# Hybrid two-layer trunk on one core: first block sums and two weights' low parts issued behind a norm's last turn on VectorE, and two HGRN transposes moved to another PSUM bank

## The chip, the core and the metric

The kernel runs on one core of a Trainium2 chip. A core has engines that run side by side, each with its own instruction queue: TensorE (PE, with weight loads shown apart as PEld) multiplies and transposes matrices, VectorE (DVE) and ScalarE (ACT) do elementwise work, SyncE (SP) issues the DMA transfers here, and GpSimd (POOL) is almost idle. The on-chip memory SBUF holds tiles of 128 partitions. TensorE writes into PSUM, which is divided into banks of 128 x 512 fp32 numbers; in this kernel a bank is one buffer of a pool.

The metric is the device time of one execution in microseconds (us). Lower is better. All times below are us unless marked otherwise.

## The reference: what is computed

Two layers over x of 512 tokens x 1024 features. Layer 0 mixes tokens by a Mamba-2 SSD mixer, layer 1 by an HGRN2 mixer with 8 heads. After each mixer come a residual layer norm, an MLP with squared ReLU (1024 to 4096 to 1024), another residual layer norm, and a gated per-layer embedding:

```python
for i in range(DEPTH):
    mix = ssd_mixer(x, ...) if i % 2 == 0 else hgrn2_mixer(x, ...)
    h = layer_norm(DEEPNORM_ALPHA * x + mix, ln_g[i, 0], ln_b[i, 0])
    h = layer_norm(DEEPNORM_ALPHA * h + sq_relu_mlp(h, mlp_w1[i], mlp_w2[i]), ln_g[i, 1], ln_b[i, 1])
    x = h + jax.nn.sigmoid(h @ ple_w_gate[i]) * (p[i] @ ple_w_proj[i])
```

An HGRN2 head carries a 128 x 128 state along the sequence. Its output is the product of decayed scores with the values inside a chunk, plus the query times the state carried in; then it is normalised per head and gated, and the heads are projected back to 1024 features.

## The kernel before

**Precision.** Each large product is done in a reduced-precision fp32 format with a split of both operands into a high and a low part. `unit` (L102) loads a 128 x 1024 weight tile into one of three `raw` buffers (issued by SP, L106), ACT casts it to its high part `whi` (L113), and DVE subtracts for the low part `wlo` (L115). `mm3` then makes three matmul passes: high by high (L119), and the two mixed ones (L120, L121). A `raw` buffer is free again when its `wlo` is through, so the load of weight n + 3 waits for the low part of weight n.

**Norms.** There are four, numbered 0 and 1 in layer 0, 2 and 3 in layer 1. A norm works on four chunks of 128 tokens. DVE takes the statistics (norm 0: L207, L208; norm 2: sums that come with the residual addition, L257, then ACT squares, L215), then scales in two passes (L223, L224). `transpose_split` then turns a chunk: for each half `q` of the features, PE makes four 128 x 128 transposes into the one bank of pool `pst`, named "pt" (L233), ACT casts the high part out of it (L237) and DVE subtracts for the low part (L238). I write a turn c0q0 for chunk 0, half 0, up to c3q1.

**MLP.** `mlp_and_gate` goes in periods. In the first period the first four tiles of w1 are multiplied in two token halves: tokens 0 to 255 need only the turns of chunks 0 and 1, tokens 256 to 511 those of chunks 2 and 3. Each tile takes 24 half passes of 256 columns for each half, 96 for the four tiles. The other tiles take 24 full passes of 512 columns. The second product (w2) is done by a block scheme with seven instead of eight products; `weight_sums` makes the sums of weight blocks on DVE (L327, L329, L330, L333) in eight `r` tiles, loaded by SP at L321, which also are weights of the second period.

**HGRN2.** The heads are done in four groups of two, `r` = 0 and 1. Group by group, with names of the code: the keys of each head (`kk`) are turned by PE (L1077, bank "pt") and copied out by ACT as `kt` (L1079); the states are `kt` times the values (L1089: head 0 in "pm", the one bank of pool `psm`, head 1 in a bank of `psy`); outputs are computed (L1107, L1109), normalised by DVE (L1117, L1119), turned (L1127, bank "pt") and split by ACT (L1128) and DVE (L1129) for the output projection. L981 is a product of the scores' part of the next group, fed by DVE through L955 and L956.

**Order of the work.** In the HGRN part the order on PE is written by hand: a group yields after each step the amount of other matmuls (projections) that is put behind it. Elsewhere a scheduler orders each engine's queue from priorities; `high_priority` moves instructions ahead (offset `SOON` = 40 for the turns' splits, `SUMS[0]` = 60 for the first block sums, `LEAD` = 100 for weights). On each engine the queue then runs in this order, and a waiting instruction holds those behind it.

Of the kernel before, what the change touches and what calls it, by code (L numbers as in the profile page):

```python
# [1 line left out]

# [1 line left out]

# [21 lines left out]
LEAD = 100  # L26
# [18 lines left out]
def trunk(ctx: ExitStack, tc, a):  # L45
# [53 lines left out]
        return v.to_broadcast(shape)  # L99


    def unit(src, lead=LEAD):  # L102
        n = src.shape[1]
        with tc.high_priority(offset=lead):
            raw = mk(raws, [P, 1024], "raw")
            nc.sync.dma_start(raw[:, :n], src)  # L106
        return split(raw[:, :n], lead)

    def split(f, lead=LEAD):
        n = f.shape[1]  # L110
        with tc.high_priority(offset=lead):
            hi = mk(whip, [P, 1024], "whi", F32R)
            nc.scalar.copy(hi[:, :n], f)  # L113
            lo = mk(wlop, [P, 1024], "wlo", F32R)
            nc.vector.tensor_sub(lo[:, :n], f, f32(hi[:, :n]))  # L115
        return hi, lo

    def mm3(out, sh, sl, mh, ml, start, stop, **kw):
# [80 lines left out]
    def layer_norm(i, c, gb, sums=None):  # L199
# [23 lines left out]
        nc.vector.scalar_tensor_tensor(src, src, mv[:, 0:1], gb[0], shift, ALU.mult)  # L223
        nc.vector.scalar_tensor_tensor(src, src, rs, gb[1], ALU.mult, ALU.add)  # L224

    def transpose_split(src, dst, c):

        sl = slice(c * P, (c + 1) * P)
        for q in range(2):
            pt = bank(pst, "pt")  # L230
            for j in range(4):
                k = 4 * q + j
                nc.tensor.transpose(pt[:, j * P : (j + 1) * P], src[:, k * P : (k + 1) * P], ident)  # L233
            v = pt.rearrange("p (j t) -> p j t", j=4)
            h = dst.hi[q][:, :, sl]
            with tc.high_priority(offset=SOON):
                nc.scalar.copy(h, v)  # L237
                nc.vector.tensor_sub(dst.lo[q][:, :, sl], v, f32(h))  # L238
            yield

    def out_part(units, n, xs, c, h, first, scale, last=False, sums=None):
# [70 lines left out]
        put("s1", a22)  # L312
        put("s4", a12)

    def weight_sums(w, lead, eng=nc.vector):

        t = [[None, None] for _ in range(4)]

        def load(i, u, src):
            t[i][u] = tmp("r", [P, 1024])  # L320
            nc.sync.dma_start(t[i][u], src)  # L321

        with tc.high_priority(offset=lead):
            for u in range(2):
                load(0, u, w[0][1][u])
                load(2, u, w[1][1][u])
                eng.tensor_sub(t[2][u], t[2][u], t[0][u])  # L327
                load(1, u, w[0][0][u])
                eng.tensor_sub(t[0][u], t[0][u], t[1][u])  # L329
                eng.tensor_add(t[1][u], t[2][u], t[1][u])  # L330
            for u in range(2):
                load(3, u, w[1][0][u])
                eng.tensor_sub(t[3][u], t[3][u], t[1][u])  # L333
        return t

    def block_product(w, blk, lead, first, after=None, turns=None, sums=None):

        t1, t2, t3, t4 = weight_sums(w, lead)  # L340
        seen = set() if first else {(i, j) for i in range(2) for j in range(2)}
        banks = {}

        def product(x, f, name, start, i, j, turns=None):
            us = [split(v) if f in (t1, t2, t3, t4) else unit(v) for v in f]
            if start:
                banks[name] = [bank(psy, "py%d" % c) if name == "x" else bank(psj, "pj") for c in range(2)]
            t = blk[x]
            for c in range(2):
                ps = banks[name][c]  # L350
                sl = slice(c * P, (c + 1) * P)
                for k in range(4):
                    hi, lo = us[k // 2]
                    ks = slice((k % 2) * 512, (k % 2 + 1) * 512)
                    w_ = hi[:, ks], lo[:, ks]
                    mm3(ps, t[:, 0, k, sl], t[:, 1, k, sl], *w_, start and k == 0, k == 3, skip_group_check=True)
                    if turns and (c, k) in ((0, 3), (1, 1)):
                        next(turns)
                d = acc[:, 2 - 2 * i + c, j * 512 : (j + 1) * 512]
                with tc.high_priority(offset=SOON if after else 0):  # L360
                    if after and f in (w[1][0], t1, t4, w[1][1]):
                        nc.vector.tensor_tensor_reduce(
                            d, ps, d, 1.0, 0.0, ALU.add, ALU.add, sums[:, 2 - 2 * i + c, j : j + 1]
                        )
                    elif (i, j) in seen:
                        nc.vector.tensor_add(d, ps, d)
                    else:
                        nc.vector.scalar_tensor_tensor(d, d, ALPHA, ps, ALU.mult, ALU.add)
            seen.add((i, j))

        p1 = lambda: product("a11", w[0][0], "x", True, 0, 0)
        p2 = lambda: product("a12", w[1][0], "z", True, 0, 0)
        p6 = lambda: product("s2", t2, "x", False, 1, 0)
        p7 = lambda: product("s3", t3, "y", True, 1, 1)
        p5 = lambda: product("s1", t1, "x", False, 1, 1)
        p4 = lambda: product("a22", t4, "y", False, 1, 0)
        p3 = lambda: product("s4", w[1][1], "x", False, 0, 1, turns)
        for f in (p1, p7, p6, p4, p5, p2, p3) if after else (p1, p2, p6, p7, p5, p4, p3):
            f()
            if after and f is p5:  # L380
                after(0), after(1)
            if after and f is p3:
                after(2), after(3)
            yield

    def mlp_and_gate(layer, h_s, last):

        w1, w2 = a[f"w1_{layer}"], a[f"w2_{layer}"]
        blocks = {}

        def hidden(g):
            names = ("a11", "a12", "a22", "s1", "s2", "s3", "s4")
            blocks[g] = {
                n: tmp("blk", [P, 2, 4, 256], F32R) if n in ("s3", "s4") else mk(b8, [P, 2, 4, 256], "b8", F32R)
                for n in names
            }
            for p in range(2):
                tiles = [4 * (2 * g + r) + 2 * p + i for r in range(2) for i in range(2)]
                us = []
                if g == p == 0:  # L400
                    for m in tiles:
                        us.append((unit(w1[m]), bank(psj, "pj")))
                        project(us[-1][0], h_s, us[-1][1], tok=slice(0, 256))
                zs = []
                for r in range(2):
                    z = mk(w4, [P, 2, T], "ab"[r])
                    for i in range(2):
                        if us:
                            u, ps = us[2 * r + i]
                            project(u, h_s, ps, tok=slice(256, 512))  # L410
                        else:
                            ps = bank(psj, "pj")
                            project(unit(w1[tiles[2 * r + i]]), h_s, ps)
                        nc.scalar.activation(z[:, i], ps, AF.Relu)
                        if i == 1:
                            nc.scalar.activation(z, z, AF.Square)
                            zs.append(z)
                            if r == 1:
                                half_blocks(blocks[g], *zs, p)
                        yield  # L420

        for g, period in enumerate(PERIODS):
            if g < 4:
                tiles = hidden(g)
            if g > 0:
                if g == 4:
                    h_s, after, turned, sums = norm(2 * layer + 1)
                    p_s = (mk(w4, [P, 2, T], "a", F32R), mk(w4, [P, 2, T], "b", F32R))
                    praw = mk(raws, [P, 1024], "raw")
                    nc.sync.dma_start(praw, a[f"pT_{layer}"].rearrange("p k t -> p (k t)"))  # L430
                    praw = praw.rearrange("p (k t) -> p k t", k=2)
                    nc.scalar.copy(p_s[0], praw)
                    nc.vector.tensor_sub(p_s[1], praw, f32(p_s[0]))
                w = [[[w2[8 * g - 8 + 4 * i + 2 * j + u] for u in range(2)] for j in range(2)] for i in range(2)]
                products = block_product(w, blocks.pop(g - 1), SUMS[g - 1], g == 1, *((after, turned(0), sums) if g == 4 else ()))
            for op in period:
                next(tiles if op == "T" else products)

# [500 lines left out]
    def hcore(h0, s, i0):  # L939
# [132 lines left out]

        kt = []
        for r in R:
            pt = bank(pst, "pt")
            for c in range(3):
                nc.tensor.transpose(pt[:, c * P : (c + 1) * P], kk[r][:, c * P : (c + 1) * P], ident)  # L1077
            kt.append(tmp("btok", [P, 3, P]))
# [5 lines left out]
        sg = lambda c, r: res[c // 2][:, c % 2, 256 + r * P : 256 + (r + 1) * P]  # L1084
        sv = []
        for r in R:
            pss = py(1) if r else bank(psm, "pm")
            for c in range(3):
                nc.tensor.matmul(pss[:, c * P : (c + 1) * P], kt[r][:, c, :], v(c, r), start=True, stop=True)  # L1089
            sv.append(tmp("pv", [P, 3, P]))  # L1090
# [31 lines left out]
            os.append(o)  # L1122
            yield FILL[3]
        for r in R:
            pt = bank(pst, "pt")
            for c in range(NCH):
                nc.tensor.transpose(pt[:, c * P : (c + 1) * P], os[r][:, c, :], ident)  # L1127
            nc.scalar.activation(s.h(i0 + r), pt, AF.Copy, scale=hnw[:, 0:1])  # L1128
# [141 lines left out]
```

## Time and profile before

| what | value |
|---|---|
| median of 3 runs | 1424.9 us (1424.33 to 1425.1) |
| the profiled execution | 1426.6 us, of it 1424.8 in the span of the profile |
| granted TensorE clock | 1.0 |
| TensorE matmuls | 1413.6 us busy, 99% |
| VectorE | 1057.4 us, 74% |
| ScalarE | 754.5 us, 53% |

A row of a timeline gives the start and the duration in us, the engine, the line, the operation, the tile written and the tiles read, how many instructions the row holds, and in brackets the idle time before it with what ended it. A row of the waits of an engine gives the line that waited, the instruction that ended the wait, the total, the number of waits and the longest. Tiles named "b" written at L237 and L238 are the turned chunks.

### The profile page before, as it was taken

How to read it: one execution, taken by the hardware profiler on the slowest of the kernel's cores; microseconds unless marked ns; L12 is line 12 of the kernel's file. 1: busy time of each engine (PE TensorE's matmuls, PEld its weight loads, DVE VectorE, ACT ScalarE, POOL GpSimd, SP SyncE). 2: the span in 40 equal slices, each digit the busy share in tenths (PEclk: the TensorE clock that was granted, in tenths of full speed). 3: DMA queues.
4: the chain of work that ended last, by engine and by line, in shares of the span. 5: the costliest groups of instructions: out<-in, count | busy, mean ns of one | idle time of the engine just before them, and what ended most of it. 6: DMA issues, size and time to landing. Idle time of an engine off the chain costs nothing.

```text
span 1424.8 us, 20421 instructions
## 1 busy us (share of the span) xinstructions
PE 1413.6 (99%) x8061; PEld 1174.6 (82%) x8061; DVE 1057.4 (74%) x1760; ACT 754.5 (53%) x1134; POOL 1.8 (0%) x12
## 2 busy tenths in 40 slices
PE   9999999999999999999999999999999999999998
PEld 7888888888888888888888887887898888888887
DVE  7988687787967667677986576678685867667873
ACT  6776454563265454545545547655555454544641
POOL 0000000000000000000000000000000000000000
PEclk9999999999999999999999999999999999999999
DMA  8432323333433444444621321222163444444231
GB/s 298 142 130 92 119 89 119 104 107 126 152 119 121 158 130 153 133 148 163 215 82 49 133 90 60 75 90 90 50 232 104 148 137 145 148 133 163 89 118 45
DMA packets 49392, 178.02 MB, mean 125 GB/s; under 512 B 5521, under 2 KB 6289, under 8 KB 49169
## 3 DMA queue, kind: packets, MB, share of 16 engines
q1 hardware_dynamic: 49296, 176.73, 36.8%
q8 instruction: 63, 1.03, 0.3%
q14 instruction: 33, 0.26, 0.1%
HBM read 174.54 MB, written 2.16 MB: 124 GB/s over the span
## 4 chain that ended last, share of the span: by engine, by line
PE 94%; DVE 3%; ACT 2%; DMA 1%; issue 0%; SPq 0%; ACTq 0%; DVEq 0%
PE pj L119 23%; PE pj L120 23%; PE pj L121 23%; PE py L119 5%; PE py L121 5%; PE py L120 5%; PE py L735 1%; PE py L741 1%; PE py L981 1%; PE pm L705 1%; DVE wlo L115 1%; PE pt L233 1%; PE pt L693 1%; DMA r<-in_w 1%; PE py L1107 0%
## 5 line engine op out<-in xcount | busy, mean ns | idle before, releaser
L113 ACT CAST whi<-raw 128x1024 fp32r<-128x1024 f32 x222 | 233.0, 1052 | 330.3 <-PE pj L120 234.1
L119 PE MATMUL pj<-b,whi 128*128 128x512 f32 (+1 forms) x1006 | 382.1, 381 | 0.7 <-ACT b L237 0.7
L120 PE MATMUL pj<-b,whi 128*128 128x512 f32 (+1 forms) x1006 | 380.6, 379 | 1.0 <-DVE b L238 1.0
L121 PE MATMUL pj<-b,wlo 128*128 128x512 f32 (+1 forms) x1006 | 379.2, 377 | 0.0
L115 DVE TENSOR_TENSOR wlo<-raw,whi 128x1024 fp32r<-128x1024 f32 x222 | 269.8, 1220 | 142.2 <-ACT whi L113 136.8
L120 PEld LDWEIGHTS pj<-b,whi 128*128 128x128 f32 x1006 | 189.4, 188 | 34.2 <-DVE b L238 1.2
L119 PEld LDWEIGHTS pj<-b,whi 128*128 128x128 f32 x1006 | 188.9, 188 | 34.1 <-ACT b L237 0.9
L121 PEld LDWEIGHTS pj<-b,wlo 128*128 128x128 f32 x1006 | 189.2, 188 | 33.6
L121 PE MATMUL pj<-whi,b 128*128 128x512 f32 x544 | 212.8, 392 | 0.0
L119 PE MATMUL pj<-whi,b 128*128 128x512 f32 x536 | 212.7, 397 | 0.0
L120 PE MATMUL pj<-wlo,b 128*128 128x512 f32 x536 | 210.2, 393 | 0.0
L121 PEld LDWEIGHTS pj<-whi,b 128*128 128x128 f32 x544 | 102.1, 188 | 20.9
L119 PEld LDWEIGHTS pj<-whi,b 128*128 128x128 f32 x536 | 100.7, 188 | 20.6 <-ACT b L1128 0.6
L120 PEld LDWEIGHTS pj<-wlo,b 128*128 128x128 f32 x536 | 100.8, 188 | 19.4
L113 ACT CAST whi<-r 128x1024 fp32r<-128x1024 f32 x72 | 75.7, 1053 | 67.8 <-PE pj L121 38.6
L115 DVE TENSOR_TENSOR wlo<-r,whi 128x1024 fp32r<-128x1024 f32 x72 | 87.6, 1219 | 23.8 <-ACT whi L113 23.2
L121 PE MATMUL py<-whi,b 128*128 128x512 f32 (+1 forms) x250 | 96.9, 388 | 0.0
L120 PE MATMUL py<-wlo,b 128*128 128x512 f32 x224 | 87.2, 389 | 0.0
L119 PE MATMUL py<-whi,b 128*128 128x512 f32 x224 | 87.1, 390 | 0.0
L121 PEld LDWEIGHTS py<-whi,b 128*128 128x128 f32 x250 | 46.9, 188 | 9.7
L634 DVE SCALAR_TENSOR_TENSOR cv<-pj,cst,cv 128x509 f32<-128x509 f32 (+2 forms) x66 | 48.7, 744 | 3.6 <-ACT cv L631 2.8
L119 PEld LDWEIGHTS py<-whi,b 128*128 128x128 f32 x224 | 42.1, 188 | 9.1 <-DVE sg L494 0.3
(303 smaller groups left out, 1864.7 us busy)
## 6 DMA issues: line engine op xcount, KB each, us to landing
raw<-in_w SPq DMA_DIRECT2D x112, 512.0 KB, 3.3
r<-in_w SPq DMA_DIRECT2D x64, 512.0 KB, 3.4
raw<-in_wssd SPq DMA_DIRECT2D x36, 512.0 KB, 3.4
a<-csd SPq DMA_DIRECT2D x16, 512.0 KB, 3.6
raw<-in_wso SPq DMA_DIRECT2D x16, 512.0 KB, 3.3
raw<-in_wg SPq DMA_DIRECT2D x16, 512.0 KB, 3.4
raw<-in_whq SPq DMA_DIRECT2D x16, 512.0 KB, 3.3
raw<-in_whvg SPq DMA_DIRECT2D x14, 512.0 KB, 3.2
```

Source lines behind the costliest of these rows:

```text
L113: nc.scalar.copy(hi[:, :n], f)
L115: nc.vector.tensor_sub(lo[:, :n], f, f32(hi[:, :n]))
L119: nc.tensor.matmul(out, sh, mh, start=start, stop=False, **kw)
L120: nc.tensor.matmul(out, sh, ml, start=False, stop=False, **kw)
L121: nc.tensor.matmul(out, sl, mh, start=False, stop=stop, **kw)
L233: nc.tensor.transpose(pt[:, j * P : (j + 1) * P], src[:, k * P : (k + 1) * P], ident)
L634: nc.vector.scalar_tensor_tensor(cv[:, d:], ps[:, : T - d], convw[:, i, k : k + 1], cv[:, d:], ALU.mult, ALU.add)
L693: nc.tensor.transpose(pt[:, c * P : (c + 1) * P], xs[:, c * P : (c + 1) * P], ident)
L705: nc.tensor.matmul(pst_[:, c * P : (c + 1) * P], btok[:, c, :], xw[:, c].rearrange("p h q -> p (h q)"), start=True, stop=True)
L735: nc.tensor.matmul(yd[64 * r : 64 * r + 64, sl], xdt[:, 2 * c + r, :], m[:, r, sl], start=True, stop=True)
L741: nc.tensor.matmul(yo[:, c * P : (c + 1) * P], pv[:, c - 1].rearrange("p h q -> p (h q)"), cm[:, c * P : (c + 1) * P], start=True, stop=True,)
L981: nc.tensor.matmul(pcs[r][bs, at : at + n], kk[r][:, ts], qs, start=True, stop=True)
```

## The change

Two edits that touch different stages.

First, `transpose_split` remembers the last DVE subtraction that it issued. `mlp_and_gate`, which is called after all four chunks of norm 0 or norm 2 have been written down, keeps that instruction as `low`, the low part of turn c3q1. `tc.issue_after(low)` tells the scheduler to put an instruction behind `low` in its engine's queue. It is used for all block sums of the first group (eight tiles, on DVE) and for the low parts of the fifth and sixth weight tile of the first period. Their loads and the ACT casts are not held.

Second, in each HGRN group the second head's key turn and the second head's output turn go to bank "pm" in place of "pt", and the first head's states to "pt" in place of "pm".

```diff
+    turned_last = []
+
+    def behind(ins):
+        return tc.issue_after(ins.ins) if ins is not None else nullcontext()
...
                 nc.scalar.copy(h, v)
-                nc.vector.tensor_sub(dst.lo[q][:, :, sl], v, f32(h))
+                turned_last[:] = [nc.vector.tensor_sub(dst.lo[q][:, :, sl], v, f32(h))]
...
             lo = mk(wlop, [P, 1024], "wlo", F32R)
-            nc.vector.tensor_sub(lo[:, :n], f, f32(hi[:, :n]))
+            with behind(after):
+                nc.vector.tensor_sub(lo[:, :n], f, f32(hi[:, :n]))
...
                 load(2, u, w[1][1][u])
-                eng.tensor_sub(t[2][u], t[2][u], t[0][u])
+                with behind(after):
+                    eng.tensor_sub(t[2][u], t[2][u], t[0][u])
...
+        low = turned_last[0]
...
-                            project(unit(w1[tiles[2 * r + i]]), h_s, ps)
+                            project(unit(w1[tiles[2 * r + i]], after=low if g == 0 and r == 0 else None), h_s, ps)
...
         for r in R:
-            pt = bank(pst, "pt")
+            pt = bank(psm, "pm") if r else bank(pst, "pt")
             for c in range(3):
...
-            pss = py(1) if r else bank(psm, "pm")
+            pss = py(1) if r else bank(pst, "pt")
...
         for r in R:
-            pt = bank(pst, "pt")
+            pt = bank(psm, "pm") if r else bank(pst, "pt")
             for c in range(NCH):
```

The scheduler moves more than the held instructions. The queue of DVE at the end of norm 0, before (L238 and L224 are the turns' low parts and the second scaling pass; `wlo` are weights' low parts; the `r` rows are block sums):

```order
L115 TENSOR_TENSOR wlo_3643<-raw_3639,whi_3641 128x1024
L221 RECIPROCAL lnrs_3362<-lnsd_3356 128x1
L223 SCALAR_TENSOR_TENSOR acc_99<-acc_99,lnmv_3355,a_3124 128x1024
L238 TENSOR_TENSOR b_554_3131<-pt_3320,b_552_3129 128x4x128
L224 SCALAR_TENSOR_TENSOR acc_99<-acc_99,lnrs_3362,b_3125 128x1024
L115 TENSOR_TENSOR wlo_3675<-raw_3671,whi_3673 128x1024
L327 TENSOR_TENSOR r_3871<-r_3871,r_3869 128x1024
L238 TENSOR_TENSOR b_553_3130<-pt_3366,b_551_3128 128x4x128
L329 TENSOR_TENSOR r_3869<-r_3869,r_3874 128x1024
L333 TENSOR_TENSOR r_3878<-r_3878,r_3865 128x1024
L238 TENSOR_TENSOR b_554_3131<-pt_3373,b_552_3129 128x4x128
```

and after the change (lines are ten or fewer higher: L244 is L238, L225 is L224, L116 is L115, L334 is L327):

```order
L222 RECIPROCAL lnrs_3362<-lnsd_3356 128x1
L224 SCALAR_TENSOR_TENSOR acc_99<-acc_99,lnmv_3355,a_3124 128x1024
L244 TENSOR_TENSOR b_554_3131<-pt_3320,b_552_3129 128x4x128
L225 SCALAR_TENSOR_TENSOR acc_99<-acc_99,lnrs_3362,b_3125 128x1024
L244 TENSOR_TENSOR b_553_3130<-pt_3366,b_551_3128 128x4x128
L244 TENSOR_TENSOR b_554_3131<-pt_3373,b_552_3129 128x4x128
L116 TENSOR_TENSOR wlo_3643<-raw_3639,whi_3641 128x1024
L116 TENSOR_TENSOR wlo_3675<-raw_3671,whi_3673 128x1024
L334 TENSOR_TENSOR r_3862<-r_3862,r_3860 128x1024
```

The fifth and sixth weight's low parts and all sums now follow the last turn. Three sums (L327, L329, L330) that stood among the steps of chunks 0 to 2 have moved there as well. On PE the turn c3q0 now stands behind 65 half passes of the first token half instead of all 96, with 13 half passes between it and c3q1 (4 before).

ACT's queue in norm 0, before (L237 is a turn's cast, L209 the square root; the last `whi` row is the sixth weight):

```order
L113 CAST whi_3641<-raw_3639 128x1024
L237 CAST b_552_3129<-pt_3267 128x4x128
L209 ACTIVATE lnsd_3303<-lnmv_3302,cst_167 128x1
L113 CAST whi_3673<-raw_3671 128x1024
L237 CAST b_551_3128<-pt_3313 128x4x128
```

and after:

```order
L210 ACTIVATE lnsd_3303<-lnmv_3302,cst_167 128x1
L113 CAST whi_3486<-raw_3484 128x1024
L113 CAST whi_3641<-raw_3639 128x1024
L113 CAST whi_3673<-raw_3671 128x1024
L243 CAST b_551_3128<-pt_3313 128x4x128
```

Here the turn's cast of chunk 1 (the second row before) has moved ahead of the weights' casts, and three weights' casts stand in a row ahead of chunk 2's first turn cast.

DVE's queue at the end of norm 2, before:

```order
L238 TENSOR_TENSOR b_1398_9048<-pt_9235,b_1396_9046 128x4x128
L224 SCALAR_TENSOR_TENSOR acc_99<-acc_99,lnrs_9280,b_9042 128x1024
L238 TENSOR_TENSOR b_1397_9047<-pt_9284,b_1395_9045 128x4x128
L327 TENSOR_TENSOR r_9780<-r_9780,r_9778 128x1024
L238 TENSOR_TENSOR b_1398_9048<-pt_9291,b_1396_9046 128x4x128
```

and after:

```order
L225 SCALAR_TENSOR_TENSOR acc_99<-acc_99,lnrs_9280,b_9042 128x1024
L244 TENSOR_TENSOR b_1397_9047<-pt_9284,b_1395_9045 128x4x128
L244 TENSOR_TENSOR b_1398_9048<-pt_9291,b_1396_9046 128x4x128
L116 TENSOR_TENSOR wlo_9561<-raw_9557,whi_9559 128x1024
L116 TENSOR_TENSOR wlo_9593<-raw_9589,whi_9591 128x1024
L334 TENSOR_TENSOR r_9780<-r_9780,r_9778 128x1024
```

The sum that stood between the last two turns' low parts is behind them. On SP five loads of `r` tiles now go ahead of the eighth and ninth weight's loads (seven went behind them before). In the HGRN part the order on PE is unchanged but in the last group, where the second output turn is spread in pieces among matmuls; only the banks differ.

More of the change, by code (lines that the diff above doesn't have):

```diff
@@ L1 @@
-from contextlib import ExitStack
+from contextlib import ExitStack, nullcontext
 import numpy as np
@@ L99, in bc, with unit @@
         return v.to_broadcast(shape)
-    def unit(src, lead=LEAD):
+    def unit(src, lead=LEAD, after=None):
         n = src.shape[1]
@@ L106, in unit, with split @@
             nc.sync.dma_start(raw[:, :n], src)
-        return split(raw[:, :n], lead)
-    def split(f, lead=LEAD):
+        return split(raw[:, :n], lead, after)
+    def split(f, lead=LEAD, after=None):
         n = f.shape[1]
@@ L313, in half_blocks, with weight_sums @@
         put("s4", a12)
-    def weight_sums(w, lead, eng=nc.vector):
+    def weight_sums(w, lead, eng=nc.vector, after=None):
         t = [[None, None] for _ in range(4)]
@@ L326, in weight_sums, with block_product @@
                 load(2, u, w[1][1][u])
-                eng.tensor_sub(t[2][u], t[2][u], t[0][u])
+                with behind(after):
+                    eng.tensor_sub(t[2][u], t[2][u], t[0][u])
                 load(1, u, w[0][0][u])
-                eng.tensor_sub(t[0][u], t[0][u], t[1][u])
-                eng.tensor_add(t[1][u], t[2][u], t[1][u])
+                with behind(after):
+                    eng.tensor_sub(t[0][u], t[0][u], t[1][u])
+                    eng.tensor_add(t[1][u], t[2][u], t[1][u])
             for u in range(2):
                 load(3, u, w[1][0][u])
-                eng.tensor_sub(t[3][u], t[3][u], t[1][u])
-        return t
-    def block_product(w, blk, lead, first, after=None, turns=None, sums=None):
-        t1, t2, t3, t4 = weight_sums(w, lead)
+                with behind(after):
+                    eng.tensor_sub(t[3][u], t[3][u], t[1][u])
+        return t
+    def block_product(w, blk, lead, first, after=None, turns=None, sums=None, low=None):
+        t1, t2, t3, t4 = weight_sums(w, lead, after=low)
         seen = set() if first else {(i, j) for i in range(2) for j in range(2)}
@@ L434, in mlp_and_gate @@
                 w = [[[w2[8 * g - 8 + 4 * i + 2 * j + u] for u in range(2)] for j in range(2)] for i in range(2)]
-                products = block_product(w, blocks.pop(g - 1), SUMS[g - 1], g == 1, *((after, turned(0), sums) if g == 4 else ()))
+                products = block_product(w, blocks.pop(g - 1), SUMS[g - 1], g == 1, *((after, turned(0), sums) if g == 4 else ()), low=low if g == 1 else None)
             for op in period:
```

## The prediction

> **What bounds the kernel now.** I read the page first, then the waits of TensorE (PE), then the timelines of the five places where a wait stands.
>
> ```profile
> span 1424.8 us, 20421 instructions
> PE 1413.6 (99%) x8061; PEld 1174.6 (82%) x8061; DVE 1057.4 (74%) x1760; ACT 754.5 (53%) x1134; POOL 1.8 (0%) x12
> ```
>
> PE is busy 99% of the span, and its granted clock is full in all forty slices. The instructions of PE stay the same work, so the change can only move the time in which PE waits. That time is listed whole:
>
> ```profile
> PE pt L1127 <- DVE b L1129: 1.5, 2, 1.0
> PE pm L153 <- DVE sq L150: 1.4, 1, 1.4
> PE pt L1077 <- ACT btok L1079: 1.4, 1, 1.4
> PE pj L120 <- DVE b L238: 1.0, 1, 1.0
> PE pj L119 <- ACT b L237: 0.7, 1, 0.7
> PE pt L233 <- DVE b L238: 0.6, 1, 0.6
> PE py L981 <- DVE qd L956: 0.4, 1, 0.4
> ```
>
> Apart from the start (L153), every large wait is at a place that the change touches: L1077 and L1127 are the HGRN turns that get another bank, L237 and L238 the last turns of the norms. A wait costs a little more than its idle time, since the end of a matmul is modelled; I count from start to start and subtract a steady step, which for a 512-column matmul is 0.23 (below, 861.38 to 861.61), for a 256-column one half of that, 0.12, and for a transpose 0.10 (863.40 to 863.71 is three).
>
> **HGRN, the second head's kk turn (group 1).** Both turns wrote bank "pt", so the second waited until ACT had copied the first out.
>
> ```profile
> 861.38 0.39 PE L120 MATMUL pj<-b,whi 128*128 128x512 f32 x1
> 861.61 0.40 PE L121 MATMUL pj<-b,wlo 128*128 128x512 f32 x1
> 863.40 0.55 PE L1077 MATMUL pt<-cst,cv 128*128 128x128 f32 x3 [1.39 <-ACT btok L1079]
> 863.71 0.48 PE L119 MATMUL pj<-b,whi 128*128 128x512 f32 x1
> 861.80 1.04 ACT L113 CAST whi<-raw 128x1024 fp32r<-128x1024 f32 x1
> 862.87 0.48 ACT L1079 COPY btok<-pt 128x384 f32<-128x384 f32 x1
> ```
>
> The loss is 863.40 - 861.61 - 0.23 = 1.56. ACT reaches the copy late, behind a weight cast. In "pm" the turn can start at 861.84. Six matmuls follow it, then the first head's states, which read that copy: 861.84 + 0.31 + 6 x 0.23 = 863.5, against the copy's end at 862.87 + 0.48 = 863.35. The wait is thus covered by six matmuls that were behind it, with 0.15 to spare; that the states now write "pt" adds only a dependence on the same copy. I take 1.5; the ends are 0.2 (the states wait instead) and 1.56. The three other groups show no wait at L1077: nothing.
>
> **HGRN, the second head's output turn (groups 2 and 3).** The same, but behind the DVE's low part of the first turn.
>
> ```profile
> 923.47 0.60 DVE L1119 SCALAR_TENSOR_TENSOR cbm<-py,hri,b 128x128 f32<-128x128 f32 x2
> 925.12 0.75 DVE L1129 SCALAR_TENSOR_TENSOR b<-pt,cst,b 128x512 fp32r<-128x512 f32 x1
> 925.06 0.39 PE L121 MATMUL pj<-b,wlo 128*128 128x512 f32 x1
> 925.92 0.66 PE L1127 MATMUL pt<-cst,cbm 128*128 128x128 f32 x4 [0.47 <-DVE b L1129]
> ```
>
> Loss 925.92 - 925.06 - 0.23 = 0.63. With its own bank the turn needs only the outputs of 923.47, done at 924.07, so it starts at 925.29. Gain 0.6.
>
> ```profile
> 970.40 0.60 DVE L1119 SCALAR_TENSOR_TENSOR cbm<-py,hri,b 128x128 f32<-128x128 f32 x2
> 972.19 0.75 DVE L1129 SCALAR_TENSOR_TENSOR b<-pt,cst,b 128x512 fp32r<-128x512 f32 x1 [1.18 <-ACT b L1128]
> 971.58 0.39 PE L121 MATMUL pj<-whi,b 128*128 128x512 f32 x1
> 972.99 0.66 PE L1127 MATMUL pt<-cst,cbm 128*128 128x128 f32 x4 [1.02 <-DVE b L1129]
> ```
>
> In group 3 the loss is 972.99 - 971.58 - 0.23 = 1.18, and the outputs are done at 971.0. But the DVE work ahead of the next intra-chunk product (L981, which already waits 0.4 for L956) runs through its own queue from 972.19 on, and comes earlier only by what ACT lets it; about half of the gain then returns as a longer wait at L981. I take 0.6, between 0.5 and 1.2. Together HGRN gives 1.5 + 0.6 + 0.6 = 2.7.
>
> **Norm 0: what leaves DVE's queue.** These rows stand between the chunks' steps; after, only the low parts of the third and fourth weight stay.
>
> ```profile
> 361.14 1.21 DVE L327 TENSOR_TENSOR r<-r,r 128x1024 f32<-128x1024 f32 x1
> 366.62 1.17 DVE L330 TENSOR_TENSOR r<-r,r 128x1024 f32<-128x1024 f32 x1
> 373.74 1.21 DVE L115 TENSOR_TENSOR wlo<-raw,whi 128x1024 fp32r<-128x1024 f32 x1
> 381.68 1.17 DVE L115 TENSOR_TENSOR wlo<-raw,whi 128x1024 fp32r<-128x1024 f32 x1
> 384.63 1.27 DVE L224 SCALAR_TENSOR_TENSOR acc<-acc,lnrs,b 128x1024 f32<-128x1024 f32 x1
> 388.09 0.68 DVE L238 TENSOR_TENSOR b<-pt,b 128x512 fp32r<-128x512 f32 x1
> 386.16 0.60 PE L233 MATMUL pt<-cst,acc 128*128 128x128 f32 x4
> 387.43 0.75 PE L119 MATMUL pj<-b,whi 128*128 128x256 f32 x4 [0.67 <-ACT b L237]
> 388.82 0.55 PE L233 MATMUL pt<-cst,acc 128*128 128x128 f32 x3 [0.65 <-DVE b L238]
> ```
>
> PE loses 387.43 - 386.16 - 4 x 0.10 = 0.87 behind the first turn of chunk 3, because all 96 half passes of the chunks before are used up, and before the second 388.82 - 0.10 (the record of its first transpose is missing) - 387.43 - 4 x 0.12 = 0.81. That is 1.7. After, three block sums (the first and the last stand above; 1.2 each, of which the next start hides a little: 3.4) and one low part (381.68, 1.1) no longer stand ahead of chunk 3's L224: it may start 4.5 earlier, at 380.1, and its first turn 1.5 later (384.63 to 386.16), at 381.6. PE's order moves that turn 31 half passes forward: 386.16 - 31 x 0.12 = 382.4. So the data are there 0.8 before PE comes. 31 passes are left to cover the turns (they end near 386.9, with the two turns), and the second turn has 13 passes (1.6) ahead of it, about as long as the first turn's cast and low part need: PE had the cast 1.27 after the turn's start (387.43), and the low part is 0.68. I take 1.5 back, with ends 0 (below) and 1.7. The two weights' low parts now run at about 386 to 388; their weights are the fifth and sixth, read when the second 96 half passes are through as well, near 398 (386.9 + 96 x 0.12). The eight sums wait for nothing before the second period.
>
> A rule on this queue: the Trainium skill, "TensorE: Matmul & The Clock Gate", section "Step-by-step: what each phase is for", says that only weight loads are pulled ahead and that "The MATMULs themselves stay in program order". The trace agrees (at 863.40 no later matmul passed the waiting turn for 1.39). By it a turn that stands 31 passes earlier blocks them all if its chunk is late; were passes free to overtake, norm 0 would give the whole 1.7 and the sum 5.5 instead of 5.3.
>
> **Norm 2.** Here only the last low part is late.
>
> ```profile
> 1038.22 7.54 DMA r<-in_w
> 1045.85 1.23 DVE L327 TENSOR_TENSOR r<-r,r 128x1024 f32<-128x1024 f32 x1 [2.27 <-DMA r<-in_w]
> 1047.00 0.68 DVE L238 TENSOR_TENSOR b<-pt,b 128x512 fp32r<-128x512 f32 x1
> 1044.33 0.59 ACT L237 CAST b<-pt 128x512 fp32r<-128x512 f32 x1 [1.47 <-PE pt L233]
> 1046.41 0.28 PE L120 MATMUL pj<-b,whi 128*128 128x256 f32 x1
> 1047.74 0.39 PE L120 MATMUL pj<-b,whi 128*128 128x256 f32 x1 [1.04 <-DVE b L238]
> ```
>
> DVE's low part waits behind a block sum whose load took 7.54. Without that sum it runs when the cast is through, at 1044.95, 2.05 earlier, and PE wanted it at 1046.53: the loss of 1047.74 - 1046.41 - 0.12 = 1.21 is gone with 0.8 to spare. On SP five loads of the sums now go ahead of the eighth and ninth weight, which wait for the two deferred low parts; the first four weights are through at about 1047.7 + 90 half passes of 0.12 = 1058.5, and the fifth to seventh take 24 passes of 0.23 each, so the eighth is read near 1075: a load of 7.54 hides. I take 1.1, with ends 0 and 1.21.
>
> POOL has no part. PE has 2 rows more only because a turn of group 4 stands in pieces. Sum: 2.7 + 1.5 + 1.1 = 5.3. The profiled execution took 1426.6 (span 1424.8) and would be 1421.3; the median of the three runs is 1424.9, so I forecast 1419.6.
>
> **Rivals.** *Norms give nothing back:* turns placed earlier in PE's order meet chunks that are late, as the rule above would have it; if chunk 3 of norm 0 came only as early as today, PE would wait 386.16 - 382.4 = 3.8. For it speaks that DVE is packed there without idle time; against it the 4.5 removed. With both norms at zero the time is 1424.9 - 2.7 = 1422.2.
>
> *HGRN gives nothing back:* the states of group 1 wait for the late copy (0.15 to spare), the chains behind groups 2 and 3 are bound by DVE. Then 1424.9 - 2.6 = 1422.3. Against it: six, and nine, ready matmuls stand behind each turn.
>
> *Slower:* on ACT the cast of the sixth weight now stands ahead of the first turn cast of chunk 2 (norm 0) and of chunk 3's squares (norm 2), and waits for its load.
>
> ```profile
> 378.36 1.05 ACT L113 CAST whi<-raw 128x1024 fp32r<-128x1024 f32 x1 [2.31 <-DMA raw<-in_w]
> 375.01 12.42 SPq L106 DMA_DIRECT2D raw<-in_w  x4
> ```
>
> That load was issued at 375.01, when the third low part was done (373.74 + 1.21), and its cast began 3.35 later. After, that low part should end near 371.5 (3.4 earlier), the load land at 374.9 and the cast end at 375.9, just when the turn's result arrives (my estimate for the turn is 375.4, and 0.6 for its transposes). There is no slack, so each us of lateness is one of PE. If the load took the 7.54 of norm 2 in place of 3.35, each norm would lose 4.2: 8.4 - 5.3 = 3.1, a time of 1428.0; it turns at 2.65 each. Against it: in norm 0 no other load runs then, and in norm 2 the sums' loads go only after the seventh weight's.
>
> *It does not do what it says:* the time stays 1424.9. The written order shows the moved rows, so this has nearly no chance.
>
> **The numbers.** 0.66 for the forecast, 0.13 for norms without gain, 0.11 for HGRN without gain, 0.07 for slower, 0.03 for no change. No difference here means within 0.2%, or 2.85 us, about what a measurement of this kernel can tell. The two half gains lie at that border (1422.05); half of their 0.24 counts as faster, half as same. So faster 0.66 + 0.12 = 0.78, same 0.12 + 0.03 = 0.15, slower 0.07. The range goes from all of the waits counted, with the 0.4 at L981 (1.56 + 0.63 + 1.18 + 1.7 + 1.21 + 0.4 = 6.7, so 1418.2), to 0.7 above the half gains, 1423.0: there one deferred cast or L981 costs a little beside.
>
> **What would show it.** Right: L1077, L1127, L237 and L238 gone from PE's list of waits, L981 longer, and the last low part of each norm directly behind its cast. Wrong: L233 waiting for DVE's L225 at chunk 2 or 3, the sixth weight's cast with idle time behind a load and a turn's cast behind it, or a wait of the states (L1099) for the copy.

## The result, and the profile after

The changed kernel takes 1419.66 us (median of 6 runs, 1419.23 to 1420.26) against 1424.93 before (6 runs, 1424.33 to 1426.6). The ratio is 0.9963 with a 95% interval of 0.9952 to 0.9974: 5.3 us, or 0.37%, faster. The forecast was 1419.6.

The head of the page and the waits of TensorE of the changed kernel (all of them; line, what ended the wait, total, number, longest):

```profile
span 1418.5 us, 20411 instructions
PE 1412.0 (100%) x8061; PEld 1174.1 (83%) x8061; DVE 1057.1 (75%) x1760; ACT 754.1 (53%) x1134; POOL 1.9 (0%) x12
```
```profile
PE pm L154 <- DVE sq L151: 1.5, 1, 1.5
PE py L991 <- DVE qd L966: 0.9, 1, 0.9
PE pt L703 <- ACT btok L672: 0.2, 1, 0.2
```

Five rows of the list before are gone: both HGRN turns (L1077, L1127) and all three at the norms' last turns (L237, L238 twice). The intra-chunk product (now L991) waits 0.9 in place of 0.4, as forecast. The row at L703 (0.2) is no new wait: it stood in the whole list before as L693, also 0.2, at about 44 us, where neither edit reaches; the prediction's list leaves it out. The intra-chunk product before and after:

```profile
982.35 0.39 PE L121 MATMUL pj<-whi,b 128*128 128x512 f32 x1
983.16 0.55 PE L981 MATMUL py<-qd,cv 128*32 128x56 f32 x28 [0.42 <-DVE qd L956]
```
```profile
976.81 0.39 PE L122 MATMUL pj<-whi,b 128*128 128x512 f32 x1
978.08 1.12 PE L991 MATMUL py<-qd,cv 128*32 128x56 f32 x63 [0.88 <-DVE qd L966]
```

From start to start, less a steady step, that is 0.58 before and 1.04 after. Counted so, the waits of the places that the change touches were 1.56 + 0.63 + 1.18 + 1.7 + 1.2 + 0.58 (the last at L981) = 6.85. What is left is 1.04 at L991 and 0.15 at one turn of norm 2, together 1.19, so 5.66 is gone by the two traces; the medians say 5.3, and the interval of the ratio allows 3.7 to 6.8.

The key turn of group 1 and what follows it, PE's and ACT's timeline of the changed kernel (start, us, engine, line):

```profile
859.59 0.39 PE L122 MATMUL pj<-b,wlo 128*128 128x512 f32 x1
859.82 0.49 PE L1087 MATMUL pm<-cst,cv 128*128 128x128 f32 x3
861.31 0.39 PE L122 MATMUL pj<-b,wlo 128*128 128x512 f32 x1
861.54 0.60 PE L1099 MATMUL pt<-a,btok 128*128 128x128 f32 x4
859.78 1.05 ACT L113 CAST whi<-raw 128x1024 fp32r<-128x1024 f32 x1
860.85 0.48 ACT L1089 COPY btok<-pt 128x384 f32<-128x384 f32 x1
```

The turn comes one step after the matmul ahead of it, although ACT still copies the first turn a microsecond later. The states start at 861.54, and the copy that they read ended at 861.33: 0.2 to spare (forecast: 0.15).

The end of norm 0, DVE, ACT and PE of the changed kernel:

```profile
380.61 1.27 DVE L225 SCALAR_TENSOR_TENSOR acc<-acc,lnrs,b 128x1024 f32<-128x1024 f32 x1
383.48 0.69 DVE L244 TENSOR_TENSOR b<-pt,b 128x512 fp32r<-128x512 f32 x1 [1.60 <-ACT b L243]
385.54 0.69 DVE L244 TENSOR_TENSOR b<-pt,b 128x512 fp32r<-128x512 f32 x1 [1.37 <-ACT b L243]
374.86 1.05 ACT L113 CAST whi<-raw 128x1024 fp32r<-128x1024 f32 x1 [1.46 <-DMA raw<-in_w]
375.99 0.59 ACT L243 CAST b<-pt 128x512 fp32r<-128x512 f32 x1
382.10 0.29 PE L121 MATMUL pj<-b,whi 128*128 128x256 f32 x1
382.22 0.60 PE L239 MATMUL pt<-cst,acc 128*128 128x128 f32 x4
384.09 0.28 PE L122 MATMUL pj<-b,wlo 128*128 128x256 f32 x1
384.22 0.66 PE L239 MATMUL pt<-cst,acc 128*128 128x128 f32 x4
```

Both turns of chunk 3 start one half pass after the matmul ahead. The last two low parts on DVE now stand with idle time before them: DVE waits for the turns, no longer PE for DVE. The deferred low parts run at 386.14, right behind. The sixth weight's cast, which the slower rival feared, starts at 374.86, after ACT stood idle 1.46 for its load, and ends just before the turn's cast of 375.99.

The end of norm 2, DVE and ACT:

```profile
1030.30 0.21 DVE L213 TENSOR_SCALAR lnmv<-lnsum 128x1 f32<-128x1 f32 x1
1037.35 0.69 DVE L244 TENSOR_TENSOR b<-pt,b 128x512 fp32r<-128x512 f32 x1 [1.43 <-ACT b L243]
1039.41 0.69 DVE L244 TENSOR_TENSOR b<-pt,b 128x512 fp32r<-128x512 f32 x1 [1.37 <-ACT b L243]
1040.02 2.35 DVE L116 TENSOR_TENSOR wlo<-raw,whi 128x1024 fp32r<-128x1024 f32 x2
1030.19 1.05 ACT L113 CAST whi<-raw 128x1024 fp32r<-128x1024 f32 x1 [0.75 <-DMA raw<-in_w]
1031.14 0.72 ACT L216 ACTIVATE cbm<-acc,lnmv 128x512 f32<-128x512 f32 x1
```

The last low part runs as soon as its cast is through, 0.6 ahead of the first held instruction, where it had waited for a sum and that sum for its load.

The ACT rows show where the 0.15 at norm 2 comes from, as far as one trace can tell. The sixth weight's cast waits for its load, and the squares of chunk 3 (L216) stand behind it. The value that they need is written by the DVE row of 1030.30 and is there by about 1030.6, but they start at 1031.14, about 0.5 later. The turn c3q0 then starts at 1036.07, 0.15 behind a steady step. So the mechanism of the slower rival did act here, at a small price.

### The profile page after: what moved, and what is told of

Read it like the earlier page. It is cut to its first block, busy times and chain, and to the rows that moved or that the text cites. A ratio compares the mean times of both kernels' runs of the same rounds, so it can differ in the third digit from the quotient of the medians.

```text
span 1418.5 us, 20411 instructions
## 1 busy us (share of the span) xinstructions
PE 1412.0 (100%) x8061; PEld 1174.1 (83%) x8061; DVE 1057.1 (75%) x1760; ACT 754.1 (53%) x1134; POOL 1.9 (0%) x12
## 4 chain that ended last, share of the span: by engine, by line
PE 98%; ACT 1%; DVE 1%; issue 0%; DVEq 0%; ACTq 0%
PE pj L120 25%; PE pj L121 25%; PE pj L122 24%; PE py L120 5%; PE py L122 5%; PE py L121 5%; PE py L745 1%; PE pt L239 1%; PE py L751 1%; PE pm L715 1%; PE py L991 1%; PE pt L703 1%; PE py L1117 0%; PE py L1119 0%; PE py L1056 0%; PE pm L154 0%
## 5 line engine op out<-in xcount | busy, mean ns | idle before, releaser
L116 DVE TENSOR_TENSOR wlo<-raw,whi 128x1024 fp32r<-128x1024 f32 x222 | 269.6, 1220 | 137.2 <-ACT whi L113 132.6
L116 DVE TENSOR_TENSOR wlo<-r,whi 128x1024 fp32r<-128x1024 f32 x72 | 87.6, 1219 | 23.8 <-ACT whi L113 23.2
```

## The experiments

Eight kernels were run. The times of each are set against the kernel before on the same chip, whose median there was 1425.8 (29 and 21 runs); differences are taken from the ratio. There is one profile of each kernel. A wait that no edit touches differs between them: the one at L703, near 44 us, was between 0.2 and 0.9. The intervals of the times often hold the forecasts of both theories. So each verdict rests on the waits, and the time only has to agree.

### Each edit alone

The banks alone (`e_banks`), without any held instruction:

```diff
-                products = block_product(..., low=low if g == 1 else None)
+                products = block_product(...)
...
-                            project(unit(w1[tiles[2 * r + i]], after=low if g == 0 and r == 0 else None), h_s, ps)
+                            project(unit(w1[tiles[2 * r + i]]), h_s, ps)
```

> Only the banks of the HGRN part are changed; sums and low parts are issued as before. Theory (each wait of TensorE is worth its start-to-start excess): HGRN gives 2.7 (1.56 + 0.63 + 0.6). In this kernel's written order of norm 2 the block sums also fall behind the last low part, though nothing asks for it, so norm 2 should give its 1.2 as well: 1424.9 - 3.9 = 1421.0; norm 0 keeps its two waits of 0.7 and 0.6. Rival (norm 2 is repaired only by the held instructions): 1422.2, with the wait of L120 for the last low part still about 1.0. Rival (the banks give nothing): 1424.9.

Measured: 1421.54, ratio 0.997 (0.9959 to 0.9981), 4.3 faster. Waits of PE:

```profile
PE pm L154 <- DVE sq L151: 1.4, 1, 1.4
PE py L991 <- DVE qd L966: 0.9, 1, 0.9
PE pt L703 <- ACT btok L672: 0.7, 1, 0.7
PE pj L120 <- ACT b L243: 0.7, 1, 0.7
PE pt L239 <- DVE b L244: 0.7, 1, 0.7
```

Norm 0's two waits of 0.7 are there, those of HGRN are gone, and norm 2's wait is gone too, though nothing holds a sum here. The first theory holds: norm 2 is repaired by the bank edit as well. In the traces the second output turn of the last group is spread among matmuls in every kernel that has it in "pm" and in no other, and DVE's order in norm 2 differs with it. That the first leads the scheduler to the second is likely, but was not tested by itself.

The held instructions alone (`e_queue`), with the banks as before:

```diff
-            pt = bank(psm, "pm") if r else bank(pst, "pt")
+            pt = bank(pst, "pt")
             for c in range(3):
...
-            pss = py(1) if r else bank(pst, "pt")
+            pss = py(1) if r else bank(psm, "pm")
...
-            pt = bank(psm, "pm") if r else bank(pst, "pt")
+            pt = bank(pst, "pt")
             for c in range(NCH):
```

> Only the sums and the two low parts are held behind the last turn; the HGRN banks are as before. Theory: norm 0 gives 1.65 and norm 2 1.2, so 1424.9 - 2.85 = 1422.05; the waits at the two HGRN turns (1.4 once, 1.5 in two) and the 0.4 at the intra-chunk product stay. Rival (the two edits are independent, so this one carries what the banks alone don't): 1419.7 + 3.9 = 1423.6 if norm 2's gain belongs to the banks.

Measured: 1423.44, ratio 0.9983 (0.9975 to 0.9992), 2.4 faster. Waits:

```profile
PE pt L1137 <- DVE b L1139: 1.5, 2, 1.0
PE pm L154 <- DVE sq L151: 1.4, 1, 1.4
PE pt L1087 <- ACT btok L1089: 1.4, 1, 1.4
PE py L991 <- DVE qd L966: 0.4, 1, 0.4
PE pt L703 <- ACT btok L672: 0.3, 1, 0.3
```

Now all waits of norms 0 and 2 are gone and all of HGRN stay. So 4.3 and 2.4 add up to 6.7, not 5.3: by the waits, the 1.2 of norm 2 is in both. Less that, 5.5 is left, which agrees with the change as a whole.

### The two halves of the held instructions

Only the sums held (`e_sums`), on top of the edit of `e_queue`:

```diff
-                            project(unit(w1[tiles[2 * r + i]], after=low if g == 0 and r == 0 else None), h_s, ps)
+                            project(unit(w1[tiles[2 * r + i]]), h_s, ps)
```

> As the run with the held instructions alone, but only the block sums are held; the fifth and sixth weight's low parts go where the scheduler puts them (ahead of the last two turns' low parts in norm 0). Theory A (the sums alone cost the time, TensorE's order follows from them): same as with both, 1422.05, the first of the last two low parts 0.7 later but covered by 20 half passes. Theory B (the two low parts are needed): norm 0 keeps about half of its loss, 0.8, so 1422.9.

Measured: 1423.19, ratio 0.9979 (0.997 to 0.9988), 3.0 faster. No wait of a norm is left. DVE and PE at the end of its norm 0:

```profile
381.31 2.34 DVE L116 TENSOR_TENSOR wlo<-raw,whi 128x1024 fp32r<-128x1024 f32 x2
383.58 0.67 DVE L244 TENSOR_TENSOR b<-pt,b 128x512 fp32r<-128x512 f32 x1
385.82 0.69 DVE L244 TENSOR_TENSOR b<-pt,b 128x512 fp32r<-128x512 f32 x1 [1.57 <-ACT b L243]
381.73 0.60 PE L239 MATMUL pt<-cst,acc 128*128 128x128 f32 x4
384.56 0.60 PE L239 MATMUL pt<-cst,acc 128*128 128x128 f32 x4
```

The two low parts stand ahead of the last turns' low parts and delay the first of them to 383.58, but it still ends at 384.25, before the second turn at 384.56, since 20 half passes stand between the two turns here. Theory A: holding the sums is enough.

Only the two low parts held (`e_lows`), on top of `e_queue`:

```diff
-                products = block_product(..., low=low if g == 1 else None)
+                products = block_product(...)
```

> As the run with the held instructions alone, but only the two weights' low parts are held; the block sums stand between the turns' steps. Theory A: norm 0 keeps its 1.65, since TensorE's order stays 96 and 4 half passes around the first turn of chunk 3; in norm 2 two sums now stand ahead of the last low part, so its loss of 1.2 stays or doubles: 1424.9 to 1426.1. Theory B (low parts carry the gain): 1422.9 or less.

Measured: 1425.01, ratio 0.9994 (0.9985 to 1.0002), 0.9 faster, but the interval includes no difference at all. Norm 0 keeps its waits of 0.7 and 0.7, as theory A has it. Norm 2 has no wait in the list, which neither theory expected. DVE and SP there:

```profile
1042.36 1.22 DVE L334 TENSOR_TENSOR r<-r,r 128x1024 f32<-128x1024 f32 x1
1043.60 1.22 DVE L337 TENSOR_TENSOR r<-r,r 128x1024 f32<-128x1024 f32 x1
1044.75 0.68 DVE L244 TENSOR_TENSOR b<-pt,b 128x512 fp32r<-128x512 f32 x1
```
```profile
1031.31 2.83 SPq L327 DMA_DIRECT2D r<-in_w  x6
1046.62 1.46 SPq L106 DMA_DIRECT2D raw<-in_w  x2
```

Two sums stand ahead of the last low part, one more than before, but their loads are issued from 1031.31, ahead of the eighth and ninth weight's, whose buffers come free only with the held low parts. The first sum so ran at 1042.36 without waiting for its load (before, it ended its wait for the load at 1045.85), and the last low part came in time.

### The two HGRN turns apart

Only the key turn (`e_kk`): the edit of `e_banks`, and the output turns back in "pt":

```diff
-            pt = bank(psm, "pm") if r else bank(pst, "pt")
+            pt = bank(pst, "pt")
             for c in range(NCH):
```

> Only the second head's key turn goes to the other bank, with the first head's states in the first; output turns, sums and low parts as before. Theory: the wait of 1.4 at the key turn goes and nothing takes its place (the states came right after six matmuls, without idle time, in the changed kernel): 1.5 faster than before, that is 1424.9 - 1.5 = 1423.4. The output turns' waits (1.5 in two), norm 0's and norm 2's stay: one block sum still stands ahead of norm 2's last low part and the sums' loads behind the ninth weight's. Rival (states wait for the copy instead): 0 to 0.3 faster.

Measured: 1423.79, ratio 0.9986 (0.9977 to 0.9995), 2.0 faster. L1087 is gone from the waits and the states do not appear; L1137 keeps 1.5 in two, norm 0 both waits, and norm 2:

```profile
PE pj L121 <- DVE b L244: 0.6, 1, 0.6
```
```profile
1042.48 1.23 DVE L334 TENSOR_TENSOR r<-r,r 128x1024 f32<-128x1024 f32 x1 [1.83 <-DMA r<-in_w]
1043.62 0.68 DVE L244 TENSOR_TENSOR b<-pt,b 128x512 fp32r<-128x512 f32 x1
```

The theory's mechanism is seen as it was told: sum waits for its load, last low part for the sum, PE for the low part. The size there was 0.8 from start to start and not 1.2, so by the waits 1.56 + 0.4 = 2.0 is gone, more than the 1.5 expected. The time agrees with 2.0, but its interval (0.7 to 3.3) holds 1.5 as well.

Only the output turn (`e_os`): the edit of `e_banks`, with the key turn and the states' banks as before.

```diff
-            pt = bank(psm, "pm") if r else bank(pst, "pt")
+            pt = bank(pst, "pt")
             for c in range(3):
...
-            pss = py(1) if r else bank(pst, "pt")
+            pss = py(1) if r else bank(psm, "pm")
```

> Only the second head's output turn goes to the other bank. Theory: groups 2 and 3 give 0.6 + 0.6, the intra-chunk product L991 waits 0.9 in place of 0.4; in this kernel's order the block sums fall behind norm 2's last low part by themselves, although their loads still go behind the ninth weight's, so norm 2 gives 1.2 too: 2.4 faster, 1422.5. If norm 2's wait stays (the loads' place decides, not the sums'), 1.2 faster, 1423.7. The key turn keeps its 1.4.

Measured: 1423.43, ratio 0.9981 (0.9972 to 0.999), 2.7 faster. L1137 is gone, L991 waits 0.9, the key turn keeps 1.4, norm 2 has no wait:

```profile
1042.94 0.69 DVE L244 TENSOR_TENSOR b<-pt,b 128x512 fp32r<-128x512 f32 x1 [1.37 <-ACT b L243]
1045.93 1.23 DVE L334 TENSOR_TENSOR r<-r,r 128x1024 f32<-128x1024 f32 x1 [2.30 <-DMA r<-in_w]
```

The sum waits for its load as long as before the change, but stands behind the last low part and harms nothing. With `e_lows` this shows that norm 2's wait needed two things, the late load and the sum's place; taking away either is enough. And it is the output turn, not the key turn, by which the bank edit repairs norm 2.

### The whole change without the two low parts

`e_banks_sums` is the changed kernel with one line back:

```diff
-                            project(unit(w1[tiles[2 * r + i]], after=low if g == 0 and r == 0 else None), h_s, ps)
+                            project(unit(w1[tiles[2 * r + i]]), h_s, ps)
```

> The whole change but for the two weights' low parts, which are not held. Theory (the sums alone let the turns stand earlier): as fast as the whole change, 1419.7, with no wait at L239 and L991 at 0.9. If the low parts of the fifth and sixth weight matter beside the banks: up to 0.8 slower than the whole change, 1420.5.

Measured: 1420.1, ratio 0.9958 (0.9944 to 0.9972), against 0.9963 (0.9952 to 0.9974) for the whole change: no difference that can be told. Its waits:

```profile
PE pm L154 <- DVE sq L151: 1.5, 1, 1.5
PE pt L703 <- ACT btok L672: 0.9, 1, 0.9
PE py L991 <- DVE qd L966: 0.9, 1, 0.9
```

Holding the two low parts is not needed for the gain.

### A late sixth weight

`e_late6` asks for the price in the slower rival. It is the changed kernel, with the sixth weight of each first period loaded twice in a row:

```diff
-    def unit(src, lead=LEAD, after=None):
+    def unit(src, lead=LEAD, after=None, twice=False):
...
-            nc.sync.dma_start(raw[:, :n], src)
+            for _ in range(2 if twice else 1): nc.sync.dma_start(raw[:, :n], src)
...
-                            project(unit(w1[tiles[2 * r + i]], after=low if g == 0 and r == 0 else None), h_s, ps)
+                            project(unit(w1[tiles[2 * r + i]], after=low if g == 0 and r == 0 else None, twice=g == 0 and r == 0 and i == 1), h_s, ps)
```

> The whole change, and the sixth weight of each first period is loaded twice in a row into the same buffer, so it lands 3.3 later. The scheduler knows of the second load and puts the weight's cast behind chunk 2's first turn cast in norm 0 and behind chunk 3's squares in norm 2. If that cast had no slack (as the slower rival of the prediction has it), each norm loses up to 3.3: 1426.3. If the order absorbs it, less than 1 in all: 1419.7 to 1420.7.

Measured: 1421.53 in a single run, above the expected range (1419.7 to 1420.7) and far below the rival's 1426.3, with nearly the same waits as `e_banks_sums` (1.4, 0.9, 0.9). Of the higher time the start explains a part: the first turn of norm 0 came at 361.3 in place of the changed kernel's 360.4, before the edit acts. The rest can't be told from chance with one run; five runs of `e_banks_sums` on this chip went from 1419.06 to 1421.51. ACT in norm 0:

```profile
376.77 0.59 ACT L243 CAST b<-pt 128x512 fp32r<-128x512 f32 x1 [2.57 <-PE pt L239]
379.00 1.05 ACT L113 CAST whi<-raw 128x1024 fp32r<-128x1024 f32 x1
```

The weight's cast comes 3.3 later than in the changed kernel (379.00 against 374.86, less the 0.8 by which this run is behind from its start) and adds no wait to PE's list, but in this kernel's order it stands behind the turn's cast. So the run shows only that another order can take in a load that is known to be late. What an unplanned delay would cost, with the cast ahead of the turn's cast, was not tried.

## Why the prediction was right, point by point

- *What bounds the kernel.* Right: PE stayed the bound, and the gain is the sum of the waits that left its list, 5.66 by the traces and 5.3 by the medians, against a forecast of 5.3. That the time came within 0.1 is luck, since the interval is 3.7 to 6.8 and single terms were off by more; what the runs bear out is the list of waits.
- *Key turn of group 1, 1.5.* Right. The whole 1.56 went; `e_kk` shows it alone, and the states did not take over the wait.
- *Output turns, 0.6 and 0.6.* Right for the first. For the second, 1.18 went and the wait at L991 grew by 0.46, from 0.58 to 1.04, so 0.7 is left; the forecast that it grows was right, its size (half of 1.18) a little high.
- *Norm 0, 1.5.* Right in time: all of the 1.7 went, and chunk 3's first turn came at 382.22 (forecast 382.4). But the step "the data are there 0.8 before PE comes" was mis-sized. L225 started at 380.61, not 380.1, and with the 1.53 from there to a turn that left 0.1. The rows that left DVE's queue were worth what was counted, but DVE did not stay packed: the way from the first statistics of chunk 1 to chunk 3's L225 took 24.1 before (360.54 to 384.63) and 20.35 after (360.26 to 380.61), 3.7 less and not 4.5. In part this is new idle time, 0.41 for a product of PE at 361.35 and 0.21 for a cast at 368.84, against one wait of 0.37 before; the rest lies in gaps too short to be listed. It took `e_sums` and `e_lows` to show which held instruction does it: the sums. The two low parts add nothing that was seen in norm 0.
- *Norm 2, 1.1.* Right in size (1.2 went, 0.15 came back at a turn, which leaves 1.05). The step "without that sum it runs when the cast is through" is what the trace shows; that the held sums are needed for it, as the sum of the terms took for granted, is wrong. The output turn's new bank alone does the same, with the order of norm 2 that comes with it. Measured apart, the bank edit is worth 4.3 and not the forecast 2.7, and the two edits overlap by 1.2. The sum is right because norm 2 is counted in it once.
- *The rivals.* Half gains: ruled out by the waits. Slower: the sixth weight's load let its cast start at 374.86 (the load was forecast for 374.9), and the cast was through at 375.91, when the turn's result came (375.33 + 0.63 = 375.96). So the sign of this rival, idle time before that cast and a turn's cast behind it, did show, and the claim that there is almost no slack is borne out; it cost nothing in norm 0 and about 0.15 in norm 2. What a longer wait would cost stays open.

## What to carry to other kernels

When one engine is busy 99% of the time, list all its waits, price each from start to start, and ask of every edit which of them it can reach; here that gave the right waits and sizes within 0.2 for each, though the time agreed better than its noise allows one to claim. Before adding up the parts of a change, ask whether a later stage is also reordered by an earlier part: in this kernel one wait of 1.2 was removed by three different single edits. A wait behind a filler on another engine (a block sum ahead of a turn's low part) can be removed at either end, by putting the filler behind or by bringing its input earlier.

## What the runs showed of the hardware that was not expected

Nothing that changes the reading. A load of 512 KB landed in 3.4 us in norm 0 of the changed kernel (issued at 371.50, with no other load issued in the 15 us before; the cast that waited for it began at 374.86), and in 7.54 us as one of seven issued in a row in norm 2 before the change. There the sum that waited for it stood ahead of the turn's low part.
